# Interleaving half of an output projection with the groups of a state space block, and regrouping the work of its helper engines

## Chip, cores and metric

The kernel runs on one core of a Trainium2 chip. The metric is device microseconds of one execution (us). The core has a matrix engine (TensorE, PE in the profile; its weight loads are PEld), VectorE (DVE), ScalarE (ACT), GpSimd (POOL) and SyncE (SP), which issues the DMAs here.

## What is computed

A decoder trunk of two layers on a sequence of 256 tokens, 1024 wide, in float32. Each layer is a gated feed-forward block, a mixer and another feed-forward block; before each block stands an RMS norm whose shift, scale and gate come from a conditioning vector times a large matrix ("modulation", six blocks of 1024 x 3072). The mixer of layer 0 is a Mamba-2 state space block, that of layer 1 attention. The change lies in the state space block, cut here to what matters:

```python
def mamba2_mixer(h, w_in, conv_w, conv_b, dt_bias, a_log, d_skip, norm_w, w_out):
    proj = h @ w_in
    z, xbc, dt = jnp.split(proj, [SSM_D_INNER, SSM_D_INNER + SSM_CONV_DIM], axis=-1)
    xbc = silu(causal_depthwise_conv4(xbc) + conv_b)
    xs, bm, cm = jnp.split(xbc, ...)                 # 2048 + 8 groups x 128 + 8 groups x 128
    dt = softplus(dt + dt_bias); a = -exp(a_log)
    # one chunk of 256 tokens, so the scan is, for each of 32 heads (4 per group):
    #   w[t, s] = (c_t . b_s) * exp(acum_t - acum_s) * dt_s   for s <= t
    #   y = w @ x + d_skip * x
    y = rmsnorm(y * silu(z), norm_w)
    return y @ w_out                                 # 2048 x 1024
```

## The kernel before, in words

All weights (some 180 MB) stream once from memory through three raw buffers (`raw`, N_RAW) in **units** of 16 blocks of 128 x 128 (1 MB, one DMA on SP's queue). A unit is worked on in halves of 8 blocks, **subs** here. Each sub is split for a float32 product made of three passes: ACT copies it in a rounded format (`hi`, L293), and the rest `raw - hi` becomes `lo` (L299 on POOL, L300 on DVE). `POOL_PART` says for each of the six phases how many sixteenths of a sub's `lo` POOL computes: 11 in the state space phase (704 of 1024 columns, DVE the other 320), none in the others. `prod` (L354) then issues three matmuls for each block: hi times the activation's high part, hi times its low part, lo times its high part (L356 to L358). So a sub is 24 matmuls of 256 columns.

`weights` (L343) is called for each block; at the first block of a sub it calls `pump` (L325), which emits the splits up to five subs ahead (AHEAD) and, between them in the order of `stream_order` (L138), the modulation steps: a DMA of 512 KB (L276) and on DVE a multiply with a running sum over 1024 columns (L306) and a small addition. `WINDOWS` (L134) says between which units how many of these 128 steps fall: 16 of them in the state space phase.

The state space phase (`mamba_units` L73, `mamba` L552) has 33 units in this order: z0, z1, a half unit dt, then for each group g the units bc(g) (the columns of b and c), x(g), and, from g = 2, z(g); then eight units o of the output projection. In the first four o units the k blocks 0 to 7 come for all eight columns m, in the last four each column m gets its k blocks 8 to 15 and is finished after 8 blocks.

The work of a group that isn't a projection hangs on **hooks**, counted in subs (h): x(g) ends at some h, its convolution (ACT L602, six instructions on DVE L607) follows at once, its SiLU (L611, L582) one sub later. `ssd_a` (L667) follows three subs after x(g) (LAG_A): on PE b times c (L670, L671), the cumulated decay of four heads spread over the partitions (L675), and four transposes of x (L680); on DVE the masked product `cbm` (L682) and the scaled x `xd` (L698). The decays are clamped at zero, two heads on DVE (`tensor_scalar` L689) and two on ACT (Relu L691), and go through two Exp on ACT (L692, L694). One sub later `weigh` (L703) multiplies the four decay tiles of 384 columns with `cbm`, alternately on DVE and POOL (L705). `ssd_b` (L708) follows six subs after x(g) (LAG_B): 16 small matmuls (L715), the skip term on DVE (L721), the gate on POOL (L723); one sub later the parts: the high part GH on ACT (L728), squares (L388, summed on POOL L390), the low part GL on DVE (L734). For the first three groups all this lies one or two subs later (LATE).

The output projection takes GH and GL; four PSUM banks are held for its eight column blocks. When a column is finished, `update` (L423) multiplies it by the row scale (L430), adds it to x (L432), squares it (L388, L390) and makes the next block's input (L412 on ACT, L413 on DVE). The next phase begins with `head` (L439), whose blocks need these inputs in the order k = 0 to 6 twice, and whose 13th block stands behind the sum of all squares (L366).

Instructions of one engine run in the order that the scheduler wrote down; a waiting instruction holds up those behind it.

Of the kernel before, what the change touches and what calls it, by code (L numbers as in the profile page):

```python
# [10 lines left out]
AF = mybir.ActivationFunctionType  # L11
# [3 lines left out]
L = 256  # L15
# [118 lines left out]
WINDOWS = ((11, 31, 32), (BASE[1] + 4, BASE[1] + 28, 16), (BASE[2] + 6, BASE[2] + 27, 40),  # L134
# [48 lines left out]
def hybrid_trunk(ctx, tc, w, mod, xt, vec, const, out, dbg=None):  # L183
# [368 lines left out]
    def mamba(j, p):  # L552
        i0 = BASE[p]
        with tc.tile_pool(name="mamba", bufs=1) as fp:
# [112 lines left out]
            def ssd_a(g, h0):  # L667
# [27 lines left out]
                for c in range(2):
                    for t in range(2):
                        h = 4 * g + 2 * c
                        dve.tensor_mul(xd[g % 2][:, c, t, :].rearrange("p (h f) -> p h f", h=2),  # L698
                                       pt[:, 256 * c + 128 * t:256 * c + 128 * t + 128]
                                       .rearrange("p (h f) -> p h f", h=2),  # L700
                                       dq[:, t, h:h + 2, None].to_broadcast([128, 2, 64]))
# [51 lines left out]
            n_o0 = M_TAGS.index(("o", 0))  # L753
            for n, (kind, g) in enumerate(M_TAGS):
                h = 2 * n + 1 + LATE.get(g, 0)
                if kind == "x":
                    at(h + LAG_B, ssd_b, g, h + LAG_B)
                elif kind == "dt":
                    at(2 * n + 2, dt_second)
                    at(2 * n + 7, dt_third)  # L760
                    at(2 * n + 9, dt_fourth)
            for n, (kind, g) in enumerate(M_TAGS):
                h = 2 * n + 1 + LATE.get(g, 0)
                if kind == "x":
                    at(h + LAG_A, ssd_a, g, h + LAG_A)
            rows = {}
            at(2 * n_o0 + 6, lambda: rows.setdefault("r", rstd_sum((ssy, ssy2), D_IN)))
            at(2 * n_o0 + 7, lambda: rstd_rows(rows["r"]))
            acc_b = []
            for n, (kind, g) in enumerate(M_TAGS):  # L770
# [3 lines left out]
                if kind != "dt":  # L774
                    st.hook = (i, lambda h=2 * n: hook(h))
# [5 lines left out]
                elif kind == "o":  # L781
                    if g == 0:
                        acc_b = [bank(True) for _ in range(4)]
                    if g == 4:
                        preload(AF.Sqrt)
                        pre_shift(j + 1)
                    for b in range(16):
                        _, k, m = ALL_UNITS[i][b]
                        o = acc_b[m % 4][:, L * (m // 4):L * (m // 4) + L]
                        prod(o, i, b, GH[:, k, :], GL[:, k, :], k == 0 and m < 4, k == 15)  # L790
                        if k == 15:
                            update(j, m, o, rb)
                else:
# [325 lines left out]
```

## Time and profile before

| what | value |
|---|---|
| median of 3 runs | 1157.6 us (1157.48 to 1158.87) |
| the profiled execution | 1158.31 us, its span 1156.5 us |
| PE, DVE, ACT, POOL busy | 96%, 80%, 53%, 20% of the span |
| mean granted clock of TensorE | 0.982 of full speed |

The profile is one execution; the span runs from the first to the last instruction, and some 1.8 us lie around it. PE is the busiest engine, but matmuls are pipelined, so its busy time also holds time in which it ran at the lower of its two clock levels. In the page's 40 slices the granted clock falls to 8 tenths in slices 11 and 12 and in the last one; the first two lie in the state space phase, which runs from 204.45 us to 466.26 us of the span.

### The profile page before, as it was taken

How to read it: one execution, taken by the hardware profiler on the slowest of the kernel's cores; microseconds unless marked ns; L12 is line 12 of the kernel's file. 1: busy time of each engine (PE TensorE's matmuls, PEld its weight loads, DVE VectorE, ACT ScalarE, POOL GpSimd, SP SyncE). 2: the span in 40 equal slices, each digit the busy share in tenths (PEclk: the TensorE clock that was granted, in tenths of full speed). 3: DMA queues.
4: the chain of work that ended last, by engine and by line, in shares of the span. 5: the costliest groups of instructions: out<-in, count | busy, mean ns of one | idle time of the engine just before them, and what ended most of it. 6: DMA issues, size and time to landing. Idle time of an engine off the chain costs nothing.

```text
span 1156.5 us, 22559 instructions
## 1 busy us (share of the span) xinstructions
PE 1108.4 (96%) x9074; PEld 1087.8 (94%) x9074; DVE 930.6 (80%) x1671; ACT 608.1 (53%) x985; POOL 227.1 (20%) x175
## 2 busy tenths in 40 slices
PE   6999999888988899999999999999999999999997
PEld 6999999877888889999999999999998999999996
DVE  7999988899998966999996699997578769655542
ACT  4464445546555545644454454445465658444541
POOL 0000004556666675000001000000112201000010
PEclk9999999999889999999999999999999999999998
DMA  9999986653454445499987569997545343655541
GB/s 353 347 343 389 338 295 243 228 185 140 150 201 146 156 155 182 151 345 383 349 320 275 185 240 349 337 359 289 188 147 182 111 146 138 228 183 183 182 146 37
DMA packets 49929, 269.02 MB, mean 233 GB/s; under 512 B 5792, under 2 KB 6560, under 8 KB 27808
## 3 DMA queue, kind: packets, MB, share of 16 engines
q1 hardware_dynamic: 49824, 267.58, 63.2%
q8 instruction: 71, 1.16, 0.4%
q14 instruction: 34, 0.28, 0.1%
HBM read 266.51 MB, written 1.05 MB: 231 GB/s over the span
## 4 chain that ended last, share of the span: by engine, by line
PE 84%; DVE 11%; ACT 2%; POOL 1%; issue 1%; DMA 0%; SPq 0%; DVEq 0%; ACTq 0%
PE bank L357 26%; PE bank L356 26%; PE bank L358 26%; DVE lo L300 3%; DVE cv L607 2%; DVE junk L306 2%; ACT hi L293 1%; PE bank L366 1%; DVE wt L705 1%; POOL sz L723 1%; PE bank L942 1%; PE bank L941 1%; PE bank L940 1%; PE bank L858 1%; DVE xs L582 1%
## 5 line engine op out<-in xcount | busy, mean ns | idle before, releaser
L357 PE MATMUL bank<-X,hi 128*128 128x256 f32 (+1 forms) x1928 | 547.1, 285 | 2.9 <-DVE X L403 2.9
L356 PE MATMUL bank<-X,hi 128*128 128x256 f32 (+1 forms) x1928 | 544.1, 285 | 2.6 <-ACT hi L293 2.6
L358 PE MATMUL bank<-X,lo 128*128 128x256 f32 (+1 forms) x1928 | 543.4, 283 | 0.0
L300 DVE TENSOR_TENSOR lo<-raw,hi 128x1024 fp32r<-128x1024 f32 (+1 forms) x361 | 417.6, 1162 | 130.8 <-ACT hi L293 129.6
L293 ACT ACTIVATE hi<-raw 128x1024 fp32r<-128x1024 f32 x361 | 377.2, 1054 | 233.6 <-PE bank L357 213.1
L356 PEld LDWEIGHTS bank<-X,hi 128*128 128x128 f32 x1928 | 369.4, 193 | 5.3 <-ACT hi L293 3.0
L357 PEld LDWEIGHTS bank<-X,hi 128*128 128x128 f32 x1928 | 368.7, 191 | 4.0 <-DVE X L403 3.7
L358 PEld LDWEIGHTS bank<-X,lo 128*128 128x128 f32 x1928 | 368.0, 191 | 0.0
L358 PE MATMUL bank<-H,lo 128*128 128x256 f32 x704 | 197.4, 280 | 0.0
L356 PE MATMUL bank<-H,hi 128*128 128x256 f32 x704 | 196.7, 279 | 0.0
L357 PE MATMUL bank<-H,hi 128*128 128x256 f32 x704 | 196.7, 279 | 0.0
L390 POOL TENSOR_TENSOR ssq<-ssq,sq 128x256 f32<-128x256 f32 x36 | 35.9, 996 | 750.8 <-ACT sq L388 750.5
L306 DVE SCALAR_TENSOR_TENSOR junk<-mraw,cb 128x1024 bf16<-128x1024 f32 x144 | 181.7, 1262 | 0.2 <-DMA mraw<-in_mod_dram 0.2
L299 POOL TENSOR_TENSOR lo<-raw,hi 128x704 fp32r<-128x704 f32 x65 | 124.4, 1920 | 61.8 <-ACT hi L293 58.5
L357 PEld LDWEIGHTS bank<-H,hi 128*128 128x128 f32 x704 | 132.6, 188 | 0.0
L358 PEld LDWEIGHTS bank<-H,lo 128*128 128x128 f32 x704 | 132.2, 188 | 0.0
L356 PEld LDWEIGHTS bank<-H,hi 128*128 128x128 f32 x704 | 131.9, 187 | 0.0
L488 ACT ACTIVATE H<-hh 128x256 fp32r<-128x256 f32 x88 | 36.3, 416 | 83.6 <-DVE hh L485 82.5
L607 DVE SCALAR_TENSOR_TENSOR cv<-bank,V,cv 128x255 f32<-128x255 f32 (+2 forms) x96 | 44.3, 474 | 4.2 <-ACT cv L602 3.6
L498 ACT ACTIVATE sg<-bank 128x256 f32<-128x256 f32 x82 | 30.3, 371 | 31.6 <-PE bank L358 31.5
L489 DVE TENSOR_TENSOR H<-hh,H 128x256 fp32r<-128x256 f32 x88 | 36.7, 420 | 8.8 <-ACT H L488 8.7
L432 DVE SCALAR_TENSOR_TENSOR x<-bank,MV,x 128x256 f32<-128x256 f32 x40 | 19.1, 481 | 30.4 <-PE bank L358 30.3
(185 smaller groups left out, 1077.2 us busy)
## 6 DMA issues: line engine op xcount, KB each, us to landing
raw<-in_w_dram SPq DMA_DIRECT2D x172, 1024.0 KB, 4.9
mraw<-in_mod_dram SPq DMA_DIRECT2D x144, 512.0 KB, 6.4
raw<-in_w_dram SPq DMA_DIRECT2D x17, 512.0 KB, 7.9
x<-in_xt_dram SPq DMA_DIRECT2D x2, 512.0 KB, 4.5
out_dram<-x SPq DMA_DIRECT2D x3, 256.0 KB, 2.3
out_dram<-x SPq DMA_DIRECT2D x2, 128.0 KB, 1.9
V<-in_vec_dram SPq DMA_DIRECT2D x1, 196.5 KB, 6.6
mask<-in_const_dram SPq DMA_DIRECT2D x1, 192.0 KB, 6.6
```

What stands on the lines that cost most here:

```text
L293: act.activation(h, r, AF.Copy)
L299: gps.tensor_sub(l[:, :c], r[:, :c], h[:, :c].bitcast(F32))
L300: ins = dve.tensor_sub(l[:, c:wd], r[:, c:wd], h[:, c:wd].bitcast(F32)).ins
L306: ins = dve.scalar_tensor_tensor(junk, mraw[SLOT["m", j, c]], 1.0, cb, op0=OP.mult, op1=OP.mult, accum_out=a).ins
L356: mm.matmul(ps, h, xh, start=start, stop=False, skip_group_check=True)
L357: mm.matmul(ps, h, xl, start=False, stop=False, skip_group_check=True)
L358: mm.matmul(ps, l, xh, start=False, stop=stop, skip_group_check=True)
L390: gps.tensor_add(total, total, s)
L488: act.activation(HH[:, m, :], h, AF.Copy)
L489: low.append(lambda: dve.tensor_sub(HL[:, m, :], h, HH[:, m, :].bitcast(F32)))
L498: act.activation(s, ps[:, :L], AF.Silu)
L607: dve.scalar_tensor_tensor(o[:, c, s:], ps[:, c, :L - s], V[:, wc + 3 - s:wc + 4 - s], o[:, c, s:], op0=OP.mult, op1=OP.add)
```

## The change

Three things are changed in the state space phase.

The order of the units: from group 2 on, each group gets a half unit p(g-2) behind z(g): the output projection of the two k blocks of group g-2 into the columns m = 0 to 3 (8 blocks). What is left of the output projection, 80 blocks, forms five units at the end, in which the columns finish four blocks apart instead of eight. Two PSUM banks are held from p0 on and two more from the first o unit. The hooks count subs exactly instead of two for each unit; LAG_A, LAG_B and LATE stay. The 16 modulation steps of the phase are put 8 between units 4 and 27 and 8 between units 28 and 33 of its 36.

POOL_PART is 0 in this phase too: DVE computes the whole `lo`.

In `ssd_a` all four heads' clamps are on ACT, `xd` is made by two instructions instead of four, and `weigh` is one instruction of two tiles (768 columns) on POOL and one on DVE instead of two and two of 384.

```diff
-ON_DVE = 2
-POOL_PART = (0, 11, 0, 0, 0, 0)
+POOL_PART = (0, 0, 0, 0, 0, 0)
+def half_out(g):
+    return [("o", k, m) for k in (2 * g, 2 * g + 1) for m in range(4)]
...
             add(("z", g), pair_unit("i", Z0 + 2 * g, Z0 + 2 * g + 1))
-    out = [("o", k, m) for k in range(8) for m in range(NK)]
-    out += [("o", k, m) for m in range(NK) for k in range(8, 16)]
-    for i in range(8):
+            add(("p", g - 2), half_out(g - 2))
+    out = half_out(6)
+    out += [("o", k, m) for m, n in ((4, 14), (5, 14), (6, 12)) for k in range(n)]
+    rest = [("o", k, 7) for k in range(16)]
+    for m in range(6):
+        out += [("o", 14, m), ("o", 15, m)] + rest[2 * m:2 * m + 2]
+    out += [("o", k, 6) for k in range(12, 16)] + rest[12:]
+    for i in range(5):
         add(("o", i), out[16 * i:16 * i + 16])
...
-WINDOWS = ((11, 31, 32), (BASE[1] + 4, BASE[1] + 28, 16), ...
+WINDOWS = ((11, 31, 32), (BASE[1] + 4, BASE[1] + 27, 8), (BASE[1] + 28, BASE[1] + 33, 8), ...
...
-                            if r < ON_DVE:
-                                dve.tensor_scalar(o, e, nac[:, t, h:h + 1], 0.0, op0=OP.add, op1=OP.min)
-                            else:
-                                act.activation(o, e, AF.Relu, bias=pac[:, t, h:h + 1], scale=-1.0)
-                act.activation(wt[:, ON_DVE:, :], wt[:, ON_DVE:, :], AF.Exp, scale=-1.0)
-                if ON_DVE:
-                    act.activation(wt[:, :ON_DVE, :], wt[:, :ON_DVE, :], AF.Exp)
+                        act.activation(o, e, AF.Relu, bias=pac[:, t, h:h + 1], scale=-1.0)
+                    if r % 2:
+                        act.activation(wt[:, r - 1:r + 1, :], wt[:, r - 1:r + 1, :], AF.Exp, scale=-1.0)
...
-                    for r in range(4):
-                        (dve, gps)[r % 2].tensor_mul(wt[:, r, :], wt[:, r, :], cbm)
+                    for q, e in ((1, gps), (0, dve)):
+                        o = wt[:, 2 * q:2 * q + 2, :]
+                        e.tensor_mul(o, o, cbm[:, None, :].to_broadcast([128, 2, 384]))
...
-            at(2 * n_o0 + 6, lambda: rows.setdefault("r", rstd_sum((ssy, ssy2), D_IN)))
-            at(2 * n_o0 + 7, lambda: rstd_rows(rows["r"]))
+            end = [sum(len(u) // SUB for u in M_UNITS[:n + 1]) - 1 for n in range(len(M_UNITS))]
+            xe = {g: end[n] + LATE.get(g, 0) for n, (kind, g) in enumerate(M_TAGS) if kind == "x"}
+            at(xe[7] + 8, lambda: rows.setdefault("r", rstd_sum((ssy, ssy2), D_IN)))
+            at(xe[7] + 9, lambda: rstd_rows(rows["r"]))
...
-                elif kind == "o":
+                elif kind in "po":
                     if g == 0:
-                        acc_b = [bank(True) for _ in range(4)]
+                        acc_b += [bank(True) for _ in range(2)]
...
-                        o = acc_b[m % 4][:, L * (m // 4):L * (m // 4) + L]
+                        o = acc_b[2 * (m // 4) + m % 2][:, L * (m % 4 // 2):L * (m % 4 // 2) + L]
```

## Rows read from the trace of the kernel before

**Rows 1.** The page's first part: busy time of each engine, its share of the span, and the number of its instructions.
```profile
PE 1108.4 (96%) x9074; PEld 1087.8 (94%) x9074; DVE 930.6 (80%) x1671; ACT 608.1 (53%) x985; POOL 227.1 (20%) x175
```

**Rows 2.** Busy time of each engine by stretch: start and end in us of the span, length, then for PE, PEld, DVE, ACT and POOL the busy us with the number of instructions, then the granted clock, the DMA engines' share and GB/s. In order: the state space phase up to the low parts of its last group; four late groups; one of them; two neighbouring subs of one group (5.20 and 2.86 us); the last seven subs of the phase; the whole phase; the feed-forward phase behind it.
```profile
204.45:436.88 232.43, 201.93 (x1567) 192.36 (x1566) 207.80 (x398) 128.53 (x216) 149.36 (x103) 0.93 0.48 171
309.87:412.35 102.48, 88.86 (x691) 85.46 (x689) 93.71 (x178) 58.17 (x98) 70.90 (x51) 0.92 0.49 174
386.57:412.35 25.78, 21.99 (x175) 21.14 (x173) 23.31 (x44) 13.97 (x24) 17.90 (x13) 0.93 0.45 165
342.75:347.95 5.20, 5.20 (x26) 5.20 (x25) 5.11 (x13) 2.63 (x6) 3.09 (x3) 0.51 0.49 197
347.95:350.81 2.86, 2.86 (x27) 2.86 (x26) 1.23 (x3) 1.97 (x3) 1.64 (x1) 1.00 0.00 0
446.48:466.26 19.78, 19.78 (x170) 19.78 (x169) 18.94 (x27) 12.03 (x20) 9.07 (x8) 1.00 0.49 168
204.45:466.26 261.81, 231.31 (x1816) 221.74 (x1815) 229.34 (x434) 145.37 (x242) 165.33 (x113) 0.93 0.48 169
466.26:654.55 188.29, 188.29 (x1596) 188.00 (x1595) 165.34 (x280) 96.18 (x142) 7.56 (x7) 1.00 0.80 300
```

**Rows 3.** The waits of PE between 217 and 436.88 us: the waiting group, whom it waited for, us in total, times, the longest.
```profile
PE bank L680 <- DVE xs L582: 13.6, 4, 3.8
PE bank L715 <- DVE wt L705: 3.7, 1, 3.7
PE bank L357 <- DVE X L403: 2.9, 2, 1.6
```

**Rows 4.** Four instructions of DVE in one late group, in order of time: start, us from the first start to the last end, then what it is (x2: two of them in a row).
```profile
387.47 3.70 DVE L300 TENSOR_TENSOR lo<-raw,hi 128x320 fp32r<-128x320 f32 x2
391.10 2.68 DVE L306 SCALAR_TENSOR_TENSOR junk<-mraw,cb 128x1024 bf16<-128x1024 f32 x1
393.71 0.68 DVE L582 SCALAR_TENSOR_TENSOR xs<-th,cv 128x512 f32<-128x512 f32 x1
```

**Rows 5.** DVE's groups by line and shape between 204.45 and 436.88 us: count, then busy us, mean ns of one, and the idle time before them with what ended it.
```profile
L300 DVE TENSOR_TENSOR lo<-raw,hi 128x320 fp32r<-128x320 f32 x55 | 48.4, 885 | 9.3 <-ACT hi L293 9.2
L306 DVE SCALAR_TENSOR_TENSOR junk<-mraw,cb 128x1024 bf16<-128x1024 f32 x16 | 26.0, 1626 | 0.0
L705 DVE TENSOR_TENSOR wt<-wt,cbm 128x384 f32<-128x384 f32 x16 | 17.2, 1103 | 0.0
L734 DVE SCALAR_TENSOR_TENSOR GL<-sz,V,GH 128x256 fp32r<-128x256 f32 x16 | 9.8, 610 | 4.5 <-ACT GH L728 4.5
L582 DVE SCALAR_TENSOR_TENSOR xs<-th,cv 128x512 f32<-128x512 f32 x8 | 9.3, 1158 | 0.0
L582 DVE SCALAR_TENSOR_TENSOR bc<-th,cv 128x512 f32<-128x512 f32 x8 | 7.1, 885 | 3.2 <-ACT th L611 3.2
L698 DVE TENSOR_TENSOR xd<-bank,dq 128x128 f32<-128x128 f32 x32 | 7.2, 277 | 0.0
L607 DVE SCALAR_TENSOR_TENSOR cv<-bank,V,cv 128x255 f32<-128x255 f32 x32 | 15.2, 475 | 3.7 <-ACT cv L602 3.6
```

**Rows 6.** The same stretch by tile: engine, operation and count, then the shortest, the median and the longest in ns, first and last start in us, and the shapes.
```profile
L300 DVE TENSOR_TENSOR lo<-raw,hi x55: 473/494/1998, 205.7 to 436.0; 128x320 fp32r<-128x320 f32 x55
L306 DVE SCALAR_TENSOR_TENSOR junk<-mraw,cb x16: 1207/1402/2709, 209.0 to 408.0; 128x1024 bf16<-128x1024 f32 x16
L705 DVE TENSOR_TENSOR wt<-wt,cbm x16: 544/1166/2045, 266.8 to 424.0; 128x384 f32<-128x384 f32 x16
L582 DVE SCALAR_TENSOR_TENSOR xs<-th,cv x8: 677/682/2171, 252.3 to 416.9; 128x512 f32<-128x512 f32 x8
L403 DVE SCALAR_TENSOR_TENSOR X<-ut,MV,X x8: 471/474/1911, 215.4 to 223.4; 128x256 fp32r<-128x256 f32 x8
L689 DVE TENSOR_SCALAR wt<-bank,nac x32: 333/406/485, 261.0 to 420.4; 128x256 f32<-128x256 f32 x16, 128x128 f32<-128x128 f32 x16
L691 ACT ACTIVATE wt<-bank,pac x32: 349/420/485, 261.1 to 420.1; 128x256 f32<-128x256 f32 x16, 128x128 f32<-128x128 f32 x16
L692 ACT ACTIVATE wt<-wt x8: 840/846/868, 263.2 to 420.5; 128x768 f32<-128x768 f32 x8
```

**Rows 7.** POOL's groups in the same stretch, columns as in rows 5.
```profile
L299 POOL TENSOR_TENSOR lo<-raw,hi 128x704 fp32r<-128x704 f32 x56 | 107.5, 1928 | 54.8 <-ACT hi L293 53.8 <-POOL ssy L390 0.9
L705 POOL TENSOR_TENSOR wt<-wt,cbm 128x384 f32<-128x384 f32 x16 | 18.1, 1149 | 16.8 <-ACT wt L692 13.8 <-issue 2.5 <-ACT wt L694 0.6
L723 POOL TENSOR_TENSOR sz<-sz,yt 128x256 f32<-128x256 f32 x16 | 15.4, 981 | 7.9 <-DVE yt L721 7.9
L390 POOL TENSOR_TENSOR ssy<-ssy,sq 128x256 f32<-128x256 f32 x14 | 11.5, 824 | 4.6 <-ACT sq L388 4.1
```

**Rows 8.** DVE over one column of the output projection's end, in order of time, columns as in rows 4.
```profile
453.61 0.41 DVE L430 TENSOR_TENSOR ut<-bank,rb 128x256 f32<-128x256 f32 x1
454.05 0.48 DVE L432 SCALAR_TENSOR_TENSOR x<-ut,MV,x 128x256 f32<-128x256 f32 x1
454.46 1.22 DVE L300 TENSOR_TENSOR lo<-raw,hi 128x1024 fp32r<-128x1024 f32 x1
455.59 0.96 DVE L413 SCALAR_TENSOR_TENSOR X<-x,MV,X 128x256 fp32r<-128x256 f32 x1
456.48 0.41 DVE L430 TENSOR_TENSOR ut<-bank,rb 128x256 f32<-128x256 f32 x1
```

**Rows 9.** DMA issues between 309.87 and 412.35 us: what, on whose queue, count, KB each, median us from issue to landing.
```profile
raw<-in_w_dram SPq DMA_DIRECT2D x12, 1024.0 KB, 4.7
mraw<-in_mod_dram SPq DMA_DIRECT2D x9, 512.0 KB, 4.9
```

More of the change, by code (lines that the diff above doesn't have):

```diff
@@ L130 @@
 PHASE_OF = [p for p in range(len(PHASES)) for _ in PHASES[p]]
[L134 removed]
+WINDOWS = ((11, 31, 32), (BASE[1] + 4, BASE[1] + 27, 8), (BASE[1] + 28, BASE[1] + 33, 8), (BASE[2] + 6, BASE[2] + 27, 40),
            (BASE[3] + 6, BASE[3] + 27, 36), (BASE[4] + 5, BASE[4] + 9, 4))
@@ L692, in ssd_a @@
-                act.activation(wt[:, ON_DVE:, :], wt[:, ON_DVE:, :], AF.Exp, scale=-1.0)
-                if ON_DVE:
-                    act.activation(wt[:, :ON_DVE, :], wt[:, :ON_DVE, :], AF.Exp)
-                for c in range(2):
[L696 to L701, printed above, removed]
+                for r in range(4):
+                    h = 4 * g + r
+                    a = pa[r // 2][:, L * (r % 2):L * (r % 2) + L]
+                    for t, o, e in ((0, wt[:, r, :256], a), (1, wt[:, r, 256:], a[:, 128:])):
+                        act.activation(o, e, AF.Relu, bias=pac[:, t, h:h + 1], scale=-1.0)
+                    if r % 2:
+                        act.activation(wt[:, r - 1:r + 1, :], wt[:, r - 1:r + 1, :], AF.Exp, scale=-1.0)
@@ L703, in weigh @@
+                for c in range(2):
+                    h = 4 * g + 2 * c
+                    dve.tensor_mul(xd[g % 2][:, c, :, :].rearrange("p t (h f) -> p t h f", h=2),
+                                   pt[:, 256 * c:256 * c + 256].rearrange("p (t h f) -> p t h f", t=2, h=2),
+                                   dq[:, :, h:h + 2, None].to_broadcast([128, 2, 2, 64]))
                 def weigh():
-                    for r in range(4):
-                        (dve, gps)[r % 2].tensor_mul(wt[:, r, :], wt[:, r, :], cbm)
+                    for q, e in ((1, gps), (0, dve)):
+                        o = wt[:, 2 * q:2 * q + 2, :]
+                        e.tensor_mul(o, o, cbm[:, None, :].to_broadcast([128, 2, 384]))
@@ L752, in mamba @@
             head(j, i0, head_z, AF.Exp)
[L753 to L765, printed above, removed]
+            end = [sum(len(u) // SUB for u in M_UNITS[:n + 1]) - 1 for n in range(len(M_UNITS))]
+            e = end[M_TAGS.index(("dt", 0))]
+            at(e + 1, dt_second)
+            at(e + 6, dt_third)
+            at(e + 8, dt_fourth)
+            xe = {g: end[n] + LATE.get(g, 0) for n, (kind, g) in enumerate(M_TAGS) if kind == "x"}
+            for g in range(8):
+                at(xe[g] + LAG_B, ssd_b, g, xe[g] + LAG_B)
+            for g in range(8):
+                at(xe[g] + LAG_A, ssd_a, g, xe[g] + LAG_A)
             rows = {}
-            at(2 * n_o0 + 6, lambda: rows.setdefault("r", rstd_sum((ssy, ssy2), D_IN)))
-            at(2 * n_o0 + 7, lambda: rstd_rows(rows["r"]))
+            at(xe[7] + 8, lambda: rows.setdefault("r", rstd_sum((ssy, ssy2), D_IN)))
+            at(xe[7] + 9, lambda: rstd_rows(rows["r"]))
             acc_b = []
@@ L773, in mamba @@
                 i = i0 + n
-                if kind != "dt":
-                    st.hook = (i, lambda h=2 * n: hook(h))
+                if len(M_UNITS[n]) == 2 * SUB:
+                    st.hook = (i, lambda h=end[n] - 1: hook(h))
                 if kind == "dt":
@@ L780, in mamba @@
                     dt_first(ps[:, :L])
-                elif kind == "o":
+                elif kind in "po":
                     if g == 0:
-                        acc_b = [bank(True) for _ in range(4)]
-                    if g == 4:
+                        acc_b += [bank(True) for _ in range(2)]
+                    if kind == "o" and g == 2:
                         preload(AF.Sqrt)
+                    if kind == "o" and g == 4:
                         pre_shift(j + 1)
-                    for b in range(16):
-                        _, k, m = ALL_UNITS[i][b]
-                        o = acc_b[m % 4][:, L * (m // 4):L * (m // 4) + L]
-                        prod(o, i, b, GH[:, k, :], GL[:, k, :], k == 0 and m < 4, k == 15)
+                    for b, (_, k, m) in enumerate(M_UNITS[n]):
+                        o = acc_b[2 * (m // 4) + m % 2][:, L * (m % 4 // 2):L * (m % 4 // 2) + L]
+                        prod(o, i, b, GH[:, k, :], GL[:, k, :], k == 0 and m % 4 < 2, k == 15)
                         if k == 15:
@@ L798, in mamba @@
                                  k == 0 and s == 0, k == NK - 1)
-                    hook(2 * n + 1)
+                    hook(end[n])
                     pv = ps.rearrange("p (c t) -> p c t", c=2)
                     if kind == "z":
-                        evac_z(g, pv, 2 * n + 1)
+                        evac_z(g, pv, end[n])
                     elif kind == "bc":
-                        conv((16 + g, 24 + g), pv, bc[g % 2], 2 * n + 1)
+                        conv((16 + g, 24 + g), pv, bc[g % 2], end[n])
                     else:
-                        conv((2 * g, 2 * g + 1), pv, xs[g % 2], 2 * n + 1)
-                hook(2 * n + 1)
+                        conv((2 * g, 2 * g + 1), pv, xs[g % 2], end[n])
+                hook(end[n])
             assert not when, when
```

5 lines of the change are left out of this document (removed).

## The prediction

> **What bounds the kernel now.** I read the page's busy times first [rows 1]: PE is busy 96% of the span, so a gain can only come where PE waits or is clocked down. The table by stretch shows where [rows 2]: in the feed-forward phase PE is busy for all of its 188.29 us at clock 1.00, while up to the last group's low parts the state space phase has PE busy 201.93 of 232.43 us at 0.93. So 30.5 us are idle there, and more is lost to the clock: behind a stall a sub takes 5.20 us at 0.51 (the lower of the two levels, 1.2 GHz), its neighbour 2.86 at 1.00 (2.4 GHz), 2.3 lost. The waits of PE [rows 3] name DVE each time; the largest, 13.6 us, is the transposes of x for DVE's SiLU, up to 3.8 us in a group. A late group lasts 25.78 us with DVE busy for 23.31 [rows 2]. **In this phase DVE, not PE, sets the pace.**
>
> Why DVE is full is seen in its durations. In one group [rows 4] two `lo` of 320 columns take 3.70 us and a modulation step 2.68, and the SiLU that PE wants comes only behind them. The shortest of these take 0.473 and 1.207 [rows 6]. Mean minus shortest, times count [rows 5, 6]: `lo` 55 x 0.41 = 22.7, modulation 16 x 0.42 = 6.7, weigh 16 x 0.56 = 8.9, SiLU of x 8 x 0.48 = 3.8 and of bc (same shape) 8 x 0.21 = 1.7, GL 16 x 0.14 = 2.2 (the shortest of its shape is 0.471, L403). That is 46 us of DVE time in which it does nothing but last longer. The convolution, which reads one operand from PSUM, has a mean of 0.475 and no such spread. So the long ones are those with both operands in SBUF, and POOL, which works in SBUF alone, is busy 149.36 us of the stretch [rows 2], 107.5 of them with `lo` [rows 7].
>
> **The change part by part.** I add up DVE to the point where group 7's low parts are done. The kernel before reaches it at 436.88, after 55 subs of PE; the new order has 59 subs there, since six p subs have come forward and it needs two fewer o subs. A sub is 19.78 / 7 = 2.83 us, so the old equivalent is 232.4 + 4 x 2.83 = 243.7 us. With these 4 added, what remains behind that point is the same for both.
>
> - *lo to DVE.* 55 instructions grow from 320 to 1024 columns: 1.22 [rows 8] minus 0.473 = 0.74 each, +40 us; four more subs are split by then, each ending 1.13 after the last, +4.5.
> - *POOL's lo goes.* Of POOL's 152.5 us [rows 7] 107.5 go, 70%. Bounds for what DVE gets back: nearly all 46 if only `lo` does it; next to nothing if the 45 us that POOL keeps hold DVE for their whole length. I take 70% of 46, **-32**, because the long `lo` and modulation in rows 4 lie beside POOL's `lo`.
> - *Clamps to ACT.* 32 tensor_scalar of 0.406 go, 13 us [rows 6]. With `xd` (32 x 0.277 become 16 of about 0.41, the price of L430's same shape in rows 8: -2.3) and weigh (16 x 0.544 become 8 of 0.94, estimated between 0.544 for 384 columns and 1.22 for 1024: -1.2) that is 16.5; neighbours on DVE overlap by under 0.1, so I take **-12**. ACT gains 32 x 0.42 = 13.4 us; it is busy 128.5 of 232. What that cover is worth: the chain from L675 to ssd_b is now 8 x 0.42 + 2 x 0.85 on ACT plus POOL's weigh, 7.0 to 7.4 us against three subs, 8.5. If ACT starts a `hi` first, PE loses up to 1 us in each of 8 groups: 0 to 8, taken as 0.
> - *POOL's weigh of 768 columns*: between 1.93 (704 columns) and 2 x 1.149 [rows 7], on POOL beside other work.
>
> The rows show first that what stretches is DVE's two-SBUF-operand work. The Trainium skill (SBUF — State Buffer, Who interferes with whom) says why: such an instruction and a GpSimd one that reads SBUF share a port pair under an exclusive lock, held for the whole instruction. By that rule alone the coming 768-column weigh speaks against the change, as does everything POOL keeps; the release would lie at the low bound, the last rival below.
>
> Sum: 207.8 + 40 + 4.5 - 32 - 12 = **208 us** of DVE. To it comes DVE's own idling: 24.6 us before (232.4 - 207.8), of which 4.5 before GL and 9.2 before `lo` [rows 5]. The first hangs on the gate on POOL, which is queued behind a 1.93 us `lo` now and will not be. I take 10 (bounds 0 and 24.6). So DVE needs 218 us against 243.7: **-25.4**.
>
> - *p subs.* The lag from x(g) to ssd_a stays three subs, so a p sub covers no wait by itself; it gives DVE 2.83 us more per group. What may be late next is p0: GL of group 0 is made behind DVE's queue, and p0 stands two subs and one ssd_a behind ssd_b(0). In the DVE sum this is a wait for work already counted: 0. If it adds, one stall of 1 to 4 us.
> - *Modulation.* 16 steps as before. Eight fall from about z6 to p5 of PE; they may hold up the SiLU of x(7) by 0 to 3 us, with room on DVE behind it. Taken as 0.
> - *Banks.* With two held, six turn; each is reused at least six allocations later, when its readers precede work that PE waits for anyway. 0, bound 1 per group.
> - *DMAs.* Eight issues of 1 MB become six of 0.5 and five of 1 MB, three more on SP's queue. They land in 4.7 us [rows 9], and three raw units are ahead: 0. Without that cover a sub would wait up to those 4.7.
> - *The end.* Columns finish 4 blocks (1.41 us) apart instead of 8. A column costs DVE 0.41 + 0.48 + 0.96 [rows 8], and a sub's `lo` 1.13 more: per sub 2 x (1.35 to 1.85) + 1.13 = 3.8 to 4.8 against PE's 2.83. Over the last four subs DVE falls behind by 4 to 8 us; the next phase's head waits for the last square 4.2 us in. PE loses 0 to 5: **+3**. Columns m and m+2 share a bank, so PE's blocks of m+2 also wait for DVE's reading of m; the same debt, earlier. By itself stands what the Trainium skill says (PSUM, PSUM bank collisions raise a hardware error), that two engines in one bank must be kept apart by semaphores; no run here shows that wait yet.
>
> Total -22.4. Against the profiled execution's 1158.31 (span 1156.5 and 1.8 around it), which is 0.7 above the median of 1157.6, that is 1136, or on the median's scale **1135 us**.
>
> **The rivals.** *DVE still idles as it did* (20%): with all 24.6 us, because its waits for ACT come from the order of work and not from its load, it needs 233: -10.7, +3, **1150**. For: its waits for `th` and `cv` are not touched. Against: 4.5 of 24.6 hang on POOL's queue.
>
> *PE becomes the bound* (12%). PE's stretch without its 30.5 idle and some 13 of slow clock (an estimate: six stalls with the 2.3 above) is 200 of 243.7. With 3 at the end and 3 at p0: -38, **1120**. For: the feed-forward phase holds PE at 100% with DVE busy 165 of 188 us and POOL 7.6 [rows 2]. Against: 208 on DVE is already more than 200.
>
> *POOL's remaining work holds DVE as much as its lo did* (7%), the slower side. With a release of 1 instead of 32, DVE needs 207.8 + 40 + 4.5 - 1 - 12 + 10 = 249: +5.6, +3, **1166**. It decides where DVE's queue meets POOL's: at weigh, which both do at about one time, and at the gate with L390. The point is a release of 10 us; under it the kernel is slower. For: DVE's weigh goes up to 2.045 beside POOL's weigh [rows 6]. Against: rows 4.
>
> **How the numbers follow.** The forecast has 58%, the three rivals 20, 12 and 7, and 3 are left for a draw between them. 0.2% (2.3 us) is about what a measurement of this kernel can tell from no change. Faster: 58 + 12 + most of 20 = 0.87; same 0.06, the edge of the idle rival and the draw; slower 0.07. The range goes from the PE rival to the idle rival, 1118 to 1151; it leaves out the slower one, the draw and the outer halves of those two, under 2 in 10. Forecast alone: 1127 to 1143.
>
> **What the new profile would show.** Right: `lo` on DVE at a mean near 1.25 for 1024 columns; modulation back to 1.25; waits of L680 for the SiLU under 1 us; clock near 0.98 in the phase; late groups (now seven subs) 24 to 25.5 us instead of 28.6; PE waiting a few us behind L432 or L413 at the end. Wrong: DVE's weigh, GL or `lo` still with means 0.4 above their shortest (then POOL's remainder was it); PE waits of 3 us and more at L680 in every group; or a head of the next phase that starts over 6 us late.

## The result and the profile after

The changed kernel takes **1129.35 us** (median of four runs, 1127.06 to 1130.21) against 1157.78 in the comparison: a ratio of 0.9752, 95% interval 0.9737 to 0.9767. The forecast was 1135, so direction and size hold, with 5.7 us more gained than said. The profiled execution took 1130.21 us, its span is 1128.4.

The page's busy times, which answer to [rows 1]:

```profile
PE 1097.0 (97%) x9074; PEld 1077.5 (95%) x9074; DVE 918.7 (81%) x1615; ACT 616.8 (55%) x1017; POOL 103.8 (9%) x102
PEclk9999999999999999999999999999999999999999
```

POOL lost 123 us of work; DVE, which took all of it over, has *less* busy time than before, 918.7 against 930.6. The clock has no weak slice left.

By stretch, columns as in [rows 2]: the state space phase up to the point that PE reaches after 59 subs; the whole phase; its last six subs; the feed-forward phase behind it.

```profile
205.43:417.66 212.23, 200.72 (x1662) 192.90 (x1661) 198.10 (x343) 140.26 (x250) 44.27 (x38) 0.99 0.54 192
205.43:437.80 232.37, 219.26 (x1817) 211.03 (x1815) 215.09 (x374) 153.66 (x273) 49.83 (x44) 0.99 0.53 188
417.66:437.80 20.14, 18.54 (x157) 18.12 (x155) 16.99 (x32) 13.40 (x24) 5.55 (x7) 1.00 0.42 151
437.80:626.42 188.62, 188.54 (x1596) 188.10 (x1595) 166.88 (x284) 96.51 (x143) 8.67 (x8) 1.00 0.80 300
```

The phase went from 261.81 [rows 2] to 232.37 us, 29.4 less; the next phase gives 0.3 back, and the two profiled executions as a whole differ by 28.1. PE's idle time in the phase fell from 30.5 to 13.1, its clock rose from 0.93 to 0.99.

PE's waits between 217 and 437.8 us, columns as in [rows 3] (L689, L691 and L718 are now what L680, L682 and L715 were):

```profile
PE bank L689 <- DVE xs L591: 5.8, 5, 2.5
PE bank L365 <- DVE cbm L691: 1.5, 1, 1.5
PE bank L718 <- DVE wt L708: 1.2, 2, 1.0
PE bank L365 <- DVE ut L439: 1.2, 1, 1.2
...
PE bank L365 <- DVE cv L616: 0.8, 1, 0.8
```

DVE's groups up to 419.93, where the last low part ends, columns as in [rows 5]:

```profile
L309 DVE TENSOR_TENSOR lo<-raw,hi 128x1024 fp32r<-128x1024 f32 x59 | 75.6, 1285 | 6.2 <-ACT hi L302 6.0
L315 DVE SCALAR_TENSOR_TENSOR junk<-mraw,cb 128x1024 bf16<-128x1024 f32 x16 | 20.0, 1248 | 0.0
L616 DVE SCALAR_TENSOR_TENSOR cv<-bank,V,cv 128x255 f32<-128x255 f32 x32 | 15.2, 475 | 0.5 <-ACT cv L611 0.4
L737 DVE SCALAR_TENSOR_TENSOR GL<-sz,V,GH 128x256 fp32r<-128x256 f32 x16 | 11.5, 726 | 1.7 <-ACT GH L731 1.7
L708 DVE TENSOR_TENSOR wt<-wt,cbm 128x768 f32<-128x768 f32 x8 | 10.4, 1296 | 1.0 <-ACT wt L698 1.0
L591 DVE SCALAR_TENSOR_TENSOR bc<-th,cv 128x512 f32<-128x512 f32 x8 | 7.9, 989 | 1.0 <-ACT th L620 0.9
L591 DVE SCALAR_TENSOR_TENSOR xs<-th,cv 128x512 f32<-128x512 f32 x8 | 7.0, 873 | 0.8 <-ACT th L620 0.8
```

`lo` of three times the columns costs 1.285 us instead of 0.885 [rows 5], and the modulation step, whose code is untouched, 1.248 instead of 1.626. By tile, columns as in [rows 6], `lo` and weigh on both engines:

```profile
L309 DVE TENSOR_TENSOR lo<-raw,hi x59: 1207/1218/2869, 206.7 to 416.6; 128x1024 fp32r<-128x1024 f32 x59
L708 POOL TENSOR_TENSOR wt<-wt,cbm x8: 1837/1982/3526, 254.3 to 409.8; 128x768 f32<-128x768 f32 x8
L708 DVE TENSOR_TENSOR wt<-wt,cbm x8: 942/958/2202, 256.9 to 412.7; 128x768 f32<-128x768 f32 x8
```

Half of all `lo` take 1.218 or less. DVE's weigh still goes up to 2.202 with POOL's piece beside it: some stretching is left where POOL still works.

### The profile page after: what moved, and what is told of

It is laid out like the page before. It is cut to its first block, busy times and chain, and to the rows that moved or that the text cites. A ratio compares the mean times of both kernels' runs of the same rounds, so it can differ in the third digit from the quotient of the medians.

```text
span 1128.4 us, 22400 instructions
## 1 busy us (share of the span) xinstructions
PE 1097.0 (97%) x9074; PEld 1077.5 (95%) x9074; DVE 918.7 (81%) x1615; ACT 616.8 (55%) x1017; POOL 103.8 (9%) x102
## 4 chain that ended last, share of the span: by engine, by line
PE 83%; DVE 9%; ACT 4%; issue 2%; POOL 1%; DMA 1%; SPq 0%; DVEq 0%; ACTq 0%; POOLq 0%
PE bank L366 26%; PE bank L365 26%; PE bank L367 26%; DVE lo L309 3%; DVE cv L616 2%; DVE junk L315 1%; ACT wt L696 1%; ACT hi L302 1%; POOL sz L726 1%; PE bank L943 1%; PE bank L942 1%; PE bank L941 1%; PE bank L859 1%; PE bank L375 1%; PE bank L899 1%
## 5 line engine op out<-in xcount | busy, mean ns | idle before, releaser
L309 DVE TENSOR_TENSOR lo<-raw,hi 128x1024 fp32r<-128x1024 f32 x361 | 442.8, 1232 | 125.4 <-ACT hi L302 124.1
L365 PE MATMUL bank<-X,hi 128*128 128x256 f32 (+1 forms) x1928 | 538.7, 282 | 4.2 <-ACT hi L302 2.6
L365 PEld LDWEIGHTS bank<-X,hi 128*128 128x128 f32 x1928 | 364.9, 191 | 7.2 <-ACT hi L302 4.7
L366 PEld LDWEIGHTS bank<-X,hi 128*128 128x128 f32 x1928 | 364.3, 189 | 1.3 <-DVE X L412 0.6
L367 PEld LDWEIGHTS bank<-X,lo 128*128 128x128 f32 x1928 | 364.1, 189 | 0.0
L365 PE MATMUL bank<-H,hi 128*128 128x256 f32 x704 | 196.4, 279 | 0.0
L315 DVE SCALAR_TENSOR_TENSOR junk<-mraw,cb 128x1024 bf16<-128x1024 f32 x144 | 175.8, 1221 | 0.0
L365 PEld LDWEIGHTS bank<-H,hi 128*128 128x128 f32 x704 | 131.7, 187 | 0.0
L365 PE MATMUL bank<-GH,hi 128*128 128x256 f32 x128 | 36.4, 284 | 2.0 <-DVE ut L439 1.2
```

Source lines behind the costliest of these rows:

```text
L309: ins = dve.tensor_sub(l[:, c:wd], r[:, c:wd], h[:, c:wd].bitcast(F32)).ins
L315: ins = dve.scalar_tensor_tensor(junk, mraw[SLOT["m", j, c]], 1.0, cb, op0=OP.mult, op1=OP.mult, accum_out=a).ins
L365: mm.matmul(ps, h, xh, start=start, stop=False, skip_group_check=True)
L366: mm.matmul(ps, h, xl, start=False, stop=False, skip_group_check=True)
L367: mm.matmul(ps, l, xh, start=False, stop=stop, skip_group_check=True)
```

## The experiments

The change has three parts: **A** the low halves to DVE, **B** the interleaving with its windows and hooks, **C** the regrouping in `ssd_a` and `weigh`. Each was run alone and each was left out; the rest takes the cause apart. "Before" ran beside each of them on the same chip, with medians from 1156.4 to 1158.5, so ratios compare best; gains and losses against "before" are taken from the one that ran beside the kernel. DVE's busy and idle time is up to the last low part (435.55 us in the kernel before, just ahead of the 436.88 of [rows 2]); phase and clock are of the profiled execution.

| kernel | median us | ratio to before, interval | phase us | clock | DVE busy / idle |
|---|---|---|---|---|---|
| before | 1157.8 | 1 | 261.8 | 0.93 | 207 / 24 |
| after (A+B+C) | 1129.35 | 0.9752, 0.9737 to 0.9767 | 232.4 | 0.99 | 200 / 14 |
| lo_only (A) | 1134.01 | 0.9800, 0.9785 to 0.9815 | 238.2 | 0.97 | 201 / 10 |
| weave_only (B) | 1164.94 | 1.0062, 1.0045 to 1.0079 | 270.0 | 0.92 | 226 / 25 |
| regroup_only (C) | 1167.63 | 1.0091, 1.0076 to 1.0106 | 271.8 | 0.91 | 198 / 43 |
| no_lo (B+C) | 1162.99 | 1.0057, 1.0039 to 1.0075 | 266.6 | 0.93 | 212 / 36 |
| no_weave (A+C) | 1132.31 | 0.9781, 0.9767 to 0.9796 | 234.4 | 0.99 | 195 / 8 |
| no_regroup (A+B) | 1134.34 | 0.9805, 0.9779 to 0.9831 | 231.4 | 0.99 | 206 / 12 |
| pool_reads | 1200.93 | 1.0376, 1.0356 to 1.0396 | 301.2 | 0.90 | 252 / 18 |
| pool_writes | 1134.53 | 0.9806, 0.9790 to 0.9821 | 238.4 | 0.96 | 200 / 10 |
| lo_share5 | 1139.28 | 0.9839, 0.9820 to 0.9857 | 242.6 | 0.98 | 199 / 25 |
| clamps_dve | 1131.53 | 0.9769, 0.9754 to 0.9784 | 232.8 | 0.99 | 205 / 13 |
| mods_later | 1129.22 | 0.9750, 0.9735 to 0.9765 | 232.0 | 0.99 | 200 / 15 |
| both_later | 1127.67 | 0.9739, 0.9724 to 0.9753 | 230.4 | 0.99 | 197 / 14 |

**lo_only**: the kernel before with one line changed.

```diff
-POOL_PART = (0, 11, 0, 0, 0, 0)
+POOL_PART = (0, 0, 0, 0, 0, 0)
```

> The kernel before with one part of the change: in the state space phase DVE computes the whole low half, POOL none of it. Theory (DVE's sum sets the pace): DVE pays 40 us more for the wider low halves and gets back 32 to 37 us that POOL's low halves cost its two-operand instructions; with 5 us less idling behind POOL's queue the time falls by 2 to 8 us, to about 1153. Rival A (the lock is nearly the whole story, the other two parts are extras): at least 15 us of the 28 come from this part alone, to 1142 or less. Rival B (DVE was full, so more work on it can only hurt): slower by 5 us or more. In the profile the theory wants the low halves of 1024 columns at a mean near 1.25 us and modulation steps near 1.25 us.

Measured: 1134.01, 23.7 of the 28.4 us, the first rival's number. The adding up of DVE had expected 2 to 8 us: with 55 x 0.74 us more work DVE is busy for *less* time (201 against 207), and its idle time fell with it, from 24 to 10. Its two rows, columns as in [rows 5], over the stretch up to 414.13:

```profile
L300 DVE TENSOR_TENSOR lo<-raw,hi 128x1024 fp32r<-128x1024 f32 x55 | 69.6, 1268 | 2.4 <-ACT hi L293 2.4
L306 DVE SCALAR_TENSOR_TENSOR junk<-mraw,cb 128x1024 bf16<-128x1024 f32 x16 | 21.8, 1361 | 0.0
```

The idle time before `lo` is 2.4 us here and was 9.3 [rows 5]: it was not DVE's own. A is the change's gain; B and C are worth 4.7 us on top.

**regroup_only**: the new `ssd_a` and `weigh` in the kernel before, POOL still with its `lo`.

```diff
-                            if r < ON_DVE:
-                                dve.tensor_scalar(o, e, nac[:, t, h:h + 1], 0.0, op0=OP.add, op1=OP.min)
...
+                        act.activation(o, e, AF.Relu, bias=pac[:, t, h:h + 1], scale=-1.0)
...
-                        (dve, gps)[r % 2].tensor_mul(wt[:, r, :], wt[:, r, :], cbm)
+                        e.tensor_mul(o, o, cbm[:, None, :].to_broadcast([128, 2, 384]))
```

> The kernel before with one part of the change: all clamps of the decays on ACT, the scaled x in two instructions for each group, the weighting in one instruction of 768 columns each on POOL and DVE. Theory (DVE's sum): 12 us of DVE go, ACT has room, so the time falls by 8 to 13 us, to about 1147. Rival (the chain from the decays to the state product gets longer by 1.7 us on ACT and by the wider POOL instruction, and DVE stays held by POOL's low halves): the time falls by less than 4 us or rises.

Measured: slower by 10 us. DVE's busy time falls by 9 us (the instructions removed are some 16 us at their shortest), but its idle time grows by 19. DVE's waits up to 446 us (who waited for whom, us in total, times, longest):

```profile
DVE cv L607 <- ACT cv L602: 15.9, 8, 3.3
DVE lo L300 <- ACT hi L293: 12.1, 10, 3.1
DVE GL L728 <- ACT GH L722: 5.8, 7, 2.0
```

In the kernel before the first of these is 3.6 [rows 5]. One of the eight, 3.23 us, in the order of time, ACT first and then DVE (start, us, what, and the idle time before it):

```profile
348.57 1.72 ACT L687 ACTIVATE wt<-bank,pac 128x256 f32<-128x256 f32 x5
...
353.45 0.56 ACT L602 ACTIVATE cv<-bank,V 128x256 f32<-128x256 f32 x1 [1.55 <-PE bank L358]
353.92 0.83 ACT L689 ACTIVATE wt<-wt 128x768 f32<-128x768 f32 x1
354.66 0.55 ACT L602 ACTIVATE cv<-bank,V 128x256 f32<-128x256 f32 x1
```

```profile
351.06 0.96 DVE L699 TENSOR_TENSOR wt<-wt,cbm 128x768 f32<-128x768 f32 x1 [0.76 <-ACT wt L689]
355.24 1.00 DVE L607 SCALAR_TENSOR_TENSOR cv<-bank,V,cv 128x255 f32<-128x255 f32 x2 [3.23 <-ACT cv L602]
```

DVE, with the clamps gone, is through at 352.0 and stands before the convolution until 355.2: ACT's start of it waits for the end of PE's projection at 353.4, and the second Exp of the clamped tiles stands between its two instructions. The time taken off DVE came back as waiting. Why PE waits longer at L680 (19.5 us, [rows 3] 13.6) was not taken apart further.

**weave_only**: units, windows and hooks of the change; `POOL_PART` and `ssd_a` as before.

```diff
+            add(("p", g - 2), half_out(g - 2))
...
+WINDOWS = ((11, 31, 32), (BASE[1] + 4, BASE[1] + 27, 8), (BASE[1] + 28, BASE[1] + 33, 8), ...
```

> The kernel before with one part of the change: half of the output projection interleaved with the groups, with the new places of the modulation steps and the exact count of subs; POOL keeps its share of the low halves, the clamps stay on both engines. Theory (DVE's sum): DVE gets 2.83 us more for each group at the cost of 0.9 us for one more low half, less about 3 us at the end: the time falls by 4 to 8 us, to about 1152. Rival A (the interleaving is the main thing: PE's idle time in the groups is filled with blocks that wait for nothing): it falls by 15 us or more. Rival B (the end of the phase is what it costs): no gain or slower.

Measured: slower by 7.3 us. The waits of ACT, then of PE, over the phase:

```profile
ACT GH L738 <- POOL sz L733: 35.7, 8, 7.2
```

```profile
PE bank L690 <- DVE xs L592: 20.0, 5, 8.5
PE bank L725 <- DVE sz L592: 5.6, 1, 5.6
```

Before, the wait of ACT was 15.5 us in 9 pieces, and PE's for x 13.6 [rows 3]. In one group POOL has itself stood 3.94 us for DVE's skip term ahead of the gate at 363.99. So the late one is DVE, with more stretch to carry (up to the last low part 78 us over the shortest of its shapes, all lines of a shape taken together; 61 before), and its lateness goes on through POOL's gate to ACT's whole queue. Which link makes the interleaving dear was not tried. Nor is it dear wherever POOL has its `lo`: with the regrouping beside it (no_lo against regroup_only) it gains some 4 us, and their intervals don't overlap.

**no_lo**, **no_weave**, **no_regroup**: the change with one part undone.

```diff
# no_lo
-POOL_PART = (0, 0, 0, 0, 0, 0)
+POOL_PART = (0, 11, 0, 0, 0, 0)
# no_weave
-            add(("p", g - 2), half_out(g - 2))
...
# no_regroup
+                            if r < ON_DVE:
+                                dve.tensor_scalar(o, e, nac[:, t, h:h + 1], 0.0, op0=OP.add, op1=OP.min)
...
```

> The changed kernel with POOL computing 704 of 1024 columns of each low half again. Theory after the first four runs (POOL's low halves hold DVE's two-operand instructions, and neither of the other two parts helps while they do): slower than before, 1165 to 1180. Rival (DVE's sum, as in the prediction): 12 us fewer on DVE and 2.83 us more time for each group still help: 1138 to 1150.

> The changed kernel without the interleaving: order of the units, modulation steps and hooks of before, with DVE's whole low halves and the regrouped work of a group. Theory (DVE's sum): 207.8 + 40 - 37 - 12 = 199 us of DVE and 14 to 20 us of idling against the 232 of before, so the time falls by 13 to 19 us, to about 1141. Rival (the interleaving is the main thing): it falls by less than 10 us.

> The changed kernel with the work of a group as before: clamps of two heads on DVE, four instructions for the scaled x, weighting in two instructions each of 384 columns on POOL and DVE. Theory (once POOL's low halves are gone PE is nearly the bound, and DVE's time has slack): within 4 us of the changed kernel, 1127 to 1133. Rival (the 12 us of DVE count, as in the prediction): 1137 or more.

Measured: 1162.99, 1132.31 and 1134.34. Without A the other two parts cost 6.6 us, about as much as B alone (7.3) and less than C alone (10.0). With A each by itself is worth little (C -1.7, B +0.3 against lo_only, neither separable from 0), both together 4.7. So the parts don't add. None of the three lies in its theory's range: no_lo is slower than before, as its theory said, but 2 us under the range; no_weave is 9 us faster than DVE's sum gave; no_regroup lies between its theory's 1133 and its rival's 1137. no_regroup has the shortest phase but one, yet lies 5 us above the change: its runs spread from 1131.2 to 1137.7, and in its profiled execution ACT waited 14.7 us for raw units in the next phase (1.2 in the change, but 12.5 in clamps_dve too, which is only 2.2 us slower than the change). What ties that loss to the regrouping stays open.

**pool_reads** and **pool_writes**: lo_only, with POOL kept as busy as before by work that nobody waits for. In the first, POOL subtracts the same 704 columns into a scratch tile; in the second it only writes zeros, four times 512 columns for each sub. Both take one modulation buffer for the scratch.

```diff
# pool_reads
+            gps.tensor_sub(st.scr[:, :704], r[:, :704], h[:, :704].bitcast(F32))
# pool_writes
+            act.activation(o[:, :1], h[:, :1].bitcast(F32), AF.Copy)
+            for _ in range(4):
+                gps.memset(o, 0.0)
```

> DVE computes the whole low half, as in the kernel with that part alone, and POOL subtracts 704 columns of each sub as before, but into a tile that nobody reads, so nothing waits for its result (modulation has four buffers instead of five to make room). Theory (POOL's reading instruction holds DVE's instructions with two operands in SBUF): DVE's stretched time is back, 30 us or more of it, the low halves at a mean of 1.5 us or more; 1160 to 1190. Rival A (PE waited for POOL's results): no slower than with that part alone, 1130 to 1138. Rival B (gate and weighting are queued behind POOL's low halves, DVE itself is not stretched): 1140 to 1150, DVE's shapes at their shortest and its idling up by 10 to 15 us.

> As the kernel in which POOL subtracts into a tile that nobody reads, but POOL instead fills that tile four times with zeros for each sub (four instructions of 512 columns, about 2 us), started by one more ACT instruction of one column; POOL only writes. Theory (only POOL's reading holds DVE): DVE's low halves stay near 1.25 us, and what is left is gate and weighting queued behind POOL: 1136 to 1150. Rival (any POOL instruction holds DVE): as with the subtraction, 1160 or more.

This is the experiment that names the cause. Over the whole span POOL is busy 233.7 us in the one, 228.1 in the other, 227.1 before. The reading one: three rows of DVE up to 474.6 us, then POOL's over the phase, columns as in [rows 5].

```profile
L303 DVE TENSOR_TENSOR lo<-raw,hi 128x1024 fp32r<-128x1024 f32 x55 | 85.1, 1551 | 1.5 <-ACT hi L294 1.5
L709 DVE TENSOR_TENSOR wt<-wt,cbm 128x384 f32<-128x384 f32 x16 | 21.3, 1353 | 0.0
L611 DVE SCALAR_TENSOR_TENSOR cv<-bank,V,cv 128x255 f32<-128x255 f32 x32 | 15.1, 471 | 0.9 <-ACT cv L606 0.9
```

```profile
L299 POOL TENSOR_TENSOR scr<-raw,hi 128x704 f32<-128x704 f32 x60 | 128.1, 2135 | 71.1 <-issue 35.8 <-ACT hi L294 22.5 <-ACT dq L645 8.2
```

The writing one, the same in the same order, DVE up to 414.6:

```profile
L306 DVE TENSOR_TENSOR lo<-raw,hi 128x1024 fp32r<-128x1024 f32 x55 | 68.2, 1243 | 2.3 <-ACT hi L294 2.3
L614 DVE SCALAR_TENSOR_TENSOR cv<-bank,V,cv 128x255 f32<-128x255 f32 x32 | 15.2, 474 | 0.9 <-ACT cv L609 0.9
L712 DVE TENSOR_TENSOR wt<-wt,cbm 128x384 f32<-128x384 f32 x16 | 9.1, 592 | 0.0
```

```profile
L302 POOL MEMSET scr<- 128x512 f32 x240 | 123.7, 527 | 33.4 <-ACT scr L300 24.9
```

POOL's reading work costs 67 us although its result is never used; as much writing costs nothing (1134.53 against 1134.01). DVE's two-SBUF-operand instructions carry it (`lo` 1.551 against 1.243, weigh 1.353 against 0.592); the convolution, with one operand from PSUM, has 0.47 in all of them. Of the 66 us between the two runs, 52 are DVE's busy time to the last low part, and the kernel is slower than expected (1160 to 1190). That POOL's reading keeps the tiles `raw` and `hi` occupied for longer explains little: ACT waited for it once, 3.7 us, the DMA queue twice, 3.8 us together.

The Trainium skill (SBUF — State Buffer, Who interferes with whom) states this split: a DVE instruction with two SBUF inputs contends with a GpSimd instruction that reads SBUF, "not with one that only writes it". These two runs agree, 1200.9 against 1134.5.

**lo_share5**: the change, with POOL given 5 of 16 parts of each `lo` instead of 11 or none.

```diff
-POOL_PART = (0, 0, 0, 0, 0, 0)
+POOL_PART = (0, 5, 0, 0, 0, 0)
```

> The changed kernel with POOL computing 5 of 16 columns (320 of 1024) of each low half, DVE the rest. Theory (POOL's instruction holds DVE for its whole length, about 1.0 us instead of 1.9): DVE saves 0.33 us for each of 65 subs and is held for more than that; the loss is about half that of 11 of 16, 1140 to 1150. Rival (a matter of balance: a small share relieves DVE): faster than the changed kernel, 1120 to 1127.

Measured: 1139.28, 9.9 slower than the change. The two halves of a `lo` over the phase:

```profile
L308 POOL TENSOR_TENSOR lo<-raw,hi 128x320 fp32r<-128x320 f32 x61 | 83.1, 1369 | 85.1 <-ACT hi L302 69.8 <-PE bank L367 5.1 <-DVE cv L616 4.9
L309 DVE TENSOR_TENSOR lo<-raw,hi 128x704 fp32r<-128x704 f32 x60 | 69.7, 1165 | 16.1 <-ACT hi L302 15.9
```

DVE's 704 columns take 1.165, hardly less than 1.285 for all 1024 (0.873 at the shortest), so POOL's 83 us take next to nothing off DVE: it is busy for 199 us against 200, and its idle time has grown from 14 to 25. Other shares were not tried.

**clamps_dve**: the change, with two heads' clamps on DVE again.

```diff
-                        act.activation(o, e, AF.Relu, bias=pac[:, t, h:h + 1], scale=-1.0)
+                        if r < 2:
+                            dve.tensor_scalar(o, e, nac[:, t, h:h + 1], 0.0, op0=OP.add, op1=OP.min)
...
```

> The changed kernel with the clamps of two of four heads back on DVE; the weighting and the scaled x stay regrouped. Prediction's price: 12 us of DVE, so 1139 or more. Theory after eight runs (DVE has the slack, PE's time hardly depends on them): within 2.5 us of the changed kernel, 1127 to 1132.

Measured: 1131.53, 2.2 us above the change, the phase 232.79 against 232.37 us; the intervals overlap, so the loss is not separable from 0. With the 32 clamps back, 13 us of instructions, DVE's busy time is 5 us longer.

**mods_later**, **both_later**: the longest stall left in the change is 2.5 us, at the transposes of x(7). DVE just before it (start, us, instruction):

```profile
398.75 1.21 DVE L315 SCALAR_TENSOR_TENSOR junk<-mraw,cb 128x1024 bf16<-128x1024 f32 x1
...
401.18 1.22 DVE L315 SCALAR_TENSOR_TENSOR junk<-mraw,cb 128x1024 bf16<-128x1024 f32 x1
...
403.23 1.22 DVE L309 TENSOR_TENSOR lo<-raw,hi 128x1024 fp32r<-128x1024 f32 x1
404.37 0.68 DVE L591 SCALAR_TENSOR_TENSOR xs<-th,cv 128x512 f32<-128x512 f32 x1
```

Two modulation steps stand in the convolution of x(7), as the prediction feared. mods_later puts the second window two units later, meant to clear that convolution; both_later also puts `ssd_a` and `ssd_b` of groups 3 to 6 one sub later.

```diff
# mods_later and both_later
-WINDOWS = (..., (BASE[1] + 4, BASE[1] + 27, 8), (BASE[1] + 28, BASE[1] + 33, 8), ...
+WINDOWS = (..., (BASE[1] + 4, BASE[1] + 28, 8), (BASE[1] + 30, BASE[1] + 34, 8), ...
# both_later
-LATE = {0: 2, 1: 2, 2: 1}
+LATE = {0: 2, 1: 2, 2: 1, 3: 1, 4: 1, 5: 1, 6: 1}
```

> The changed kernel with its second eight modulation steps put between units 30 and 34 instead of 28 and 33 (and the first eight up to 28 instead of 27). Theory (the stall of 2.5 us before the last group's transposes is the SiLU of x(7) queued behind these steps): it goes, and with it 1 to 3 us, 1126 to 1128. Rival (the steps then meet the updates at the end of the phase, where DVE is full): what is gained there is lost before the next phase, 1129 to 1132.

> As the kernel with the later modulation steps, and groups 3 to 6 do their state space work one sub later (LATE). Theory (PE's remaining waits for the SiLU of x, 5.8 us in all, are a matter of a short lag): they fall under 1.5 us and the time by 3 to 6 us, 1123 to 1126. Rival (DVE is full in these groups, so the wait only moves, to the state product or to the blocks of the output projection): 1127 to 1131.

Measured: 1129.22 and 1127.67. mods_later does not clear the convolution: the window's eight steps now start from 378 to 411 us instead of 370 to 406, and its fourth and fifth stand where the sixth and seventh stood. DVE there, the convolution starting at 396.07:

```profile
394.28 1.76 DVE L315 SCALAR_TENSOR_TENSOR junk<-mraw,cb 128x1024 bf16<-128x1024 f32 x1
...
396.99 1.21 DVE L315 SCALAR_TENSOR_TENSOR junk<-mraw,cb 128x1024 bf16<-128x1024 f32 x1
...
402.09 0.69 DVE L591 SCALAR_TENSOR_TENSOR xs<-th,cv 128x512 f32<-128x512 f32 x1
```

PE's wait for x(7) is 1.85 us for 2.50, all its waits at L689 5.4 for 5.8, the time as it was. So this run doesn't decide whether the stall hangs on the modulation steps. In both_later the waits for the SiLU of x are gone, though a step still stands in that convolution (at 391.54), and others stand in their place (PE's waits over its phase):

```profile
PE bank L375 <- POOL ssy L399: 2.8, 1, 2.8
PE bank L718 <- DVE cv L616: 2.3, 3, 1.0
```

It has the lowest median of all, 1.7 us under the change, but its interval overlaps the change's: not shown to be faster.

## Why the prediction was right, and where its steps were off

**PE waits for DVE, and POOL's reading is what makes DVE late: shown**, by lo_only and by pool_reads against pool_writes. That the sum of DVE's busy time sets the length is not: regroup_only and clamps_dve speak against it. The slower rival (POOL's remainder holds DVE as much as its `lo` did) is out: weigh and GL keep some stretch, 8 x 0.354 and 16 x 0.255 us (mean over shortest), which is 7 us and not 46. What the prediction gave for it was a misreading: DVE's weigh of 2.045 did not lie beside POOL's weigh but beside POOL's `lo`, and beside POOL's weigh no piece took more than 1.36. In the kernel before, DVE's longest piece and a late one, each with POOL's instruction beside it:

```profile
268.44 2.04 DVE L705 TENSOR_TENSOR wt<-wt,cbm 128x384 f32<-128x384 f32 x1
268.06 2.00 POOL L299 TENSOR_TENSOR lo<-raw,hi 128x704 fp32r<-128x704 f32 x1
...
398.50 1.36 DVE L705 TENSOR_TENSOR wt<-wt,cbm 128x384 f32<-128x384 f32 x1
398.19 1.26 POOL L705 TENSOR_TENSOR wt<-wt,cbm 128x384 f32<-128x384 f32 x1
```

**lo to DVE and POOL's lo goes: right.** The six shapes that made 46 us of stretch come to 59 x 0.078 + 16 x 0.041 + 8 x 0.354 + 16 x 0.255 + 8 x 0.196 + 8 x 0.312 = 16 us, a release of 30 where 32 was taken. The same sum over all of DVE's shapes fell from 61 to 24: 37, since shapes that the prediction left out were stretched too. That is 5 of the 10 us by which DVE at PE's 59 subs is under the forecast, 198.1 against 208; most of the rest is the regrouping, which took some 16 us off DVE's sum where 12 were taken.

**Clamps to ACT, -12: the step that failed.** The term stands for the whole regrouping. Its instructions went, but as time the clamps alone are worth 2.2 us, not separable from 0 (clamps_dve); the whole is worth 5.0 on top of the other two parts (no_regroup), 1.7, not separable from 0, on top of A alone (no_weave against lo_only), and with POOL's `lo` in place it costs 10 (regroup_only). The prediction took the time off DVE's sum, as if the sum were the length; what comes off DVE where it waits for ACT or PE next is waited for, in regroup_only 9 us off its busy time against 19 more of idling.

**The total is near in part by luck.** By the prediction's terms A alone gains 32 + 14.6 - 40 = 7 us, and the other two parts the remaining 16. Measured, A gains 23.7 and the others 4.7 on top: one part was put far too low, the others too high, and the errors partly cancel.

**Idle 10: it is 14.1** (212.23 - 198.10), inside its bounds. But A alone brings it to 10; the argument by the gate on POOL explained 4.5 of it, and the idle time before `lo`, 9.3 before and 2.4 in lo_only (6.2 again in the change), was the larger piece. The idle rival (1150) fails by this. Busy and idle together are 212.2 against 218: this 5.8 is the error of the whole.

**The PE rival (1120) came closer than its 12% says.** It had 200 us of PE to the equal point; PE is busy 200.7 there, at a clock of 0.99. But 11.5 us of idle time are left, so the result lies between the two cases.

**p subs, 0:** against no_weave the change is 3.0 us faster, with intervals that just touch. **Modulation, 0 (0 to 3):** the stall is there, 2.5 us, inside the range; whether the steps cause it stays open, since mods_later left one in the convolution and one just ahead of it. **Banks and DMAs, 0:** two waits look like a bank's earlier reader, L365 behind DVE's `cbm`, 1.5 us, and behind its `cv`, 0.8 us, inside the bound of 1 per group in sum; none for a raw unit shows among PE's.

**The end, +3 (0 to 5):** 29.38 us lay behind the equal point before, less four subs 18.1; now it is 20.14, and the next phase is 0.3 longer: +2.4. Of this 1.2 is PE waiting at L365 for DVE's L439, the reading of a column that shares its bank, the wait that no row had shown.

Of the signs, `lo` (1.285), modulation (1.248) and the clock (0.99) came as written, and POOL's weigh (2.295 on average) at the upper end of its range. The transposes of x on PE at the start and at the end of four late groups:

```profile
314.43 0.66 PE L689 MATMUL bank<-ident,xs 128*128 128x128 f32 x4 [0.76 <-DVE xs L591]
...
405.11 0.66 PE L689 MATMUL bank<-ident,xs 128*128 128x128 f32 x4 [2.50 <-DVE xs L591]
```

Four groups of seven subs in 90.7 us are 22.7 each, below the 24 to 25.5 said; six subs took 25.6 before (102.48 / 4 [rows 2]). Of the five waits there three are under 1 us, as said, the others 1.95 and 2.50.

## What to carry to other kernels

Before giving POOL a share of an elementwise job, compare what it takes off DVE with how much longer DVE's other two-SBUF-operand instructions become: here 704 of 1024 columns saved 0.74 us a sub and cost more than that in stretch and waiting, and 320 columns did not pay either. Look in the trace at the mean against the shortest of one shape; here a spread on such instructions and none on the convolution, which reads PSUM, pointed to POOL's reads. Don't price a moved instruction by an engine's sum alone: the same regrouping, some 16 us off DVE, changed the time by +10 us in one surrounding, by -5.0 in another and by -1.7, not separable from 0, in a third.

## What the runs showed that was not expected

POOL's writes are free for DVE here: 240 memsets, 123.7 us of POOL, moved the time by 0.5 us, within the intervals. POOL's reads cost more than twice the whole gain of the change: 128 us of them, with nobody waiting, made the kernel 67 us slower, and with PE waiting its clock in the phase fell from 0.97 to 0.90. And POOL suffers as well: the 704-column subtraction took it 2.135 us on average beside a DVE that subtracts all columns, against 1.928 [rows 7].
